# Experts' outputs accumulated in four PSUM banks by float32r one-hot products, picks for two experts at once, one conditional block per expert

## The chip, the cores and the metric

The kernel runs on one core of a Trainium2 chip. The metric is the device time of one execution in microseconds, the median over several runs. An execution under the profiler gives a span (first to last instruction) and its own device time, which is a little above the span.

## The reference

All arithmetic is float32. A first block has two hybrid layers (projections, attention, retention, an mLSTM, output projection). A second block has one layer: a mixer (attention and a gated recurrence), and then a mixture of experts over 256 tokens, which is what the change touches:

```
xn = rms_norm(x, norm2_g)                          # 256 tokens x 1024
logits = xn @ w_router + b_router                  # 32 experts
top_v, top_i = top_k(logits, 4); gates = softmax(top_v)
for each expert e, over the tokens that picked it:
    g = min(xn @ w_gate[e] + b_gate[e], 7)
    u = clip(xn @ w_up[e] + b_up[e], -7, 7)
    y = (g * sigmoid(1.702 g) * (u + 1)) @ w_down[e] + b_down[e]
x = x + sum over a token's 4 experts of gate * y
out = rms_norm(x, final_g)
```

Each of the three weights of an expert is 1024 x 1024 float32, 4 MB, so the 32 experts read 403 MB. 256 tokens with 4 experts each are 32 tokens an expert on average.

## The kernel before

**The first part** (the two layers and the mixer, up to about 480 us) works through weight tiles that are split into two float32r parts, three products each (`mm3`, lines 368 to 370). The change leaves it alone, but for the place at which two buffers are handed back (`give`).

**Weights** come in tiles of 1 MB (128 partitions x 2048 numbers), each by one DMA that SyncE (SP) issues, into a ring of numbered slots (`slot`, tiles named `s`). `give(...)` returns slots and issues the next loads of a list `order` in that order; `release(i)` gives back the slot of load i. In the experts' part 19 slots turn over. An expert uses twelve tiles: four of w_gate, four of w_up, four of w_down.

**One expert** (lines 1303 to 1333) has a capacity of 64 tokens. `pick` makes a one-hot matrix from the tokens' ranks (VectorE), gathers the tokens' rows by float32 matmuls (`xg`), copies them out (ScalarE), transposes them in four 128x128 pieces (`tr`) and scales them into `xT`. `up` multiplies xT by the gate tiles (PSUM bank `g`) and the up tiles (bank `u`). Since only 64 rows of output are wanted, the 128x128 array is used in two halves of 64 columns: matmuls come in pairs that write partitions 0 to 63 and 64 to 127 at the same time. I call this the 64-column form. Each float32 matmul stands in the trace as two instructions (PE) with two weight loads (PEld), so a product of 16 matmuls has 32. The bias is one float32r matmul in the full 128x128 form in the middle of each product. `gated` computes the activation in five steps on VectorE and ScalarE, `down` transposes the result (`tr`), copies it out as `hT` (ScalarE, line 1253) and multiplies by the down tiles (bank `y`). For every two experts `place` builds the transposed and gated one-hot matrices (bank `st`), and `add_pair` multiplies them by the two outputs: four float32 matmuls of 128x512 with two instructions each (bank `cb`), added to x by VectorE (line 1269).

**Experts with over 64 tokens** go through conditional blocks: `more_up` (line 1278) after the first half, `more_down` (line 1284) after the second, nested up to three deep. Every engine loads the expert's token count and branches twice per expert; `foresee` puts a hint for the PE's branch into its stream. In this data two experts take the blocks, expert 1 and expert 29.

**Order.** A scheduler sets the order of the instructions on each engine, so in PE's stream matmuls of one product are interleaved with the picks of the next expert and with the adds. SP's loads for w_gate and w_up stand behind the first conditional block, those for w_down behind the second.

Of the kernel before, what the change touches and what calls it, by code (L numbers as in the profile page):

```python
# [26 lines left out]
def _col_layout():  # L27
    at, off = {}, 0
    for name, n in (
        ("norm0", 8), ("norm1", 8), ("y0", 4), ("y1", 4), ("cw0", 16), ("cw1", 16), ("cb0", 4), ("cb1", 4),  # L30
        ("n1g", 8), ("final", 8), ("cw2", 16), ("cb2", 4), ("ba", 8), ("bi", 8), ("lam", 8), ("og", 8), ("n2g", 8),
    ):
        at[name] = (off, n)
        off += n
    return at, off
# [62 lines left out]
def _prep(i):  # L98
# [29 lines left out]
    z["b_down"] = a["b_down_2"][0][:, :768].reshape(32, 3, 256).transpose(1, 0, 2).reshape(96, 256)  # L128
    z["b_down_end"] = a["b_down_2"][0][:, 768:].reshape(32, 2, 128).transpose(1, 0, 2).reshape(64, 128)
# [21 lines left out]
    put("n2g", a["norm2_g_2"][0])  # L151
    z["cols"] = c
# [43 lines left out]
def _build(tc, T, out):  # L196
# [577 lines left out]
    def mixer(xt):  # L774
# [242 lines left out]
        give(13, 15, 16, 17, 18, 21)  # L1017
# [15 lines left out]
        give(4, 5, 6, 7, 11)  # L1033
# [40 lines left out]
    ew = ctx.enter_context(tc.tile_pool(name="ew", bufs=1))  # L1074
    t22, t23 = slot(22), slot(23)
    xh = slot(12).rearrange("p (a b) -> p a b", a=2)
    bias = ew.tile([128, 1024], F32R, name="bias")
    xg, th = t22[:, 0:512], t22[:, 512:1024]
    more_h = [t22[:, 1024:1536], t22[:, 1536:2048], ew.tile([128, 512], F32, name="more")]
    ys, xTs = ([t23[:, o + 512 * k:o + 512 * k + 512] for k in range(2)] for o in (0, 1024))  # L1080
    nc.scalar.dma_start(rbc[0:96, :], T["b_down"])
    gates, rank = (sm(n, 2, 32, bufs=1) for n in ("gates", "rank"))
    count = small.tile([1, 32], I32, name="count", bufs=1)

    t14 = slot(14)

    def split_bias():

        b = t14[:, 256:1280]
        nc.scalar.dma_start(b, T["bias"])  # L1090
        S.activation(bias, b, AF.Copy)
        for p in (slice(32, 64), slice(96, 128)):
            V.tensor_tensor(bias[p], b[p], bias[p].bitcast(F32), op=OP.subtract)

    def router():
        xT = slot(10).rearrange("p (k t) -> p k t", k=8)
        wr, br = t14[:, 0:256], t14[:, 1536:1568]
        lg, mr = (t14[:, o:o + 72].rearrange("p (a b) -> p a b", a=2) for o in (1568, 1640))
        mask, m8, sel, nv = (t14[:, o:o + n].rearrange("p (a b) -> p a b", a=2)
                             for o, n in ((1712, 64), (1776, 16), (1792, 16), (1808, 4)))  # L1100
        nc.scalar.dma_start(wr, T["w_router"])
        load_row(br, "br")
        r, _ = x_stats(1e-5, xh, False, True)
        tt = [bank(n) for n in ("xg", "tr", "st", "y")]
# [11 lines left out]
        for hf in range(2):  # L1116
            for kt in range(8):
                ins = PE.matmul(t[:, 32 * hf:32 * hf + 32], xT[:, kt, 128 * hf:128 * hf + 128], wr.rearrange("p (k e) -> p k e", k=8)[:, kt, :],
                          start=kt == 0, stop=kt == 7)
            busy(ins, 8 if hf else 4, bank("cb", 2))  # L1120
# [21 lines left out]
        busy(ins, 4, bank("cb", 2))  # L1142
# [4 lines left out]

    def last_bias():

        t = bank("tr")  # L1150
        gx = ew.tile([128, 2, 192], F32, name="hotw")[:, :, 0:96]
        V.tensor_copy(gx.rearrange("p a (q e) -> p a q e", q=3), gates[:, :, None, :].to_broadcast([128, 2, 3, 32]))
        for hf in range(2):
            PE.transpose(t[0:96, 128 * hf:128 * hf + 128], gx[:, hf, :], ident)
        V.tensor_copy(one[0:96, :], t[0:96, 0:256])
        for q, w, o in ((0, rbc, 0), (1, rbc, 256), (2, rbc, 512), (0, b_down, 768), (1, b_down, 896)):
            p, n = slice(32 * q, 32 * q + 32), w.shape[-1]
            t = bank("cb", 2)
            for hf in range(2):
                PE.matmul(t[:, n * hf:n * hf + n], one[p, 128 * hf:128 * hf + 128], w[p, :], start=True, stop=True)  # L1160
            d = x[:, :, o:o + n]
            V.tensor_tensor(d, d, two(t[:, 0:2 * n]), op=OP.add)

    router()
    b_down = before[0:64, :]
    nc.scalar.dma_start(b_down, T["b_down_end"])
    four = lambda v: v.rearrange("p (c s t) -> p c s t", c=4, s=2)
    gain = cols[:, COLS["n2g"][0]:COLS["n2g"][0] + 8].rearrange("p (s c) -> p c s", s=2)

    def ranks(e, j):  # L1170
        if not j:
            return rank[:, :, e]
        r = sm("rj", 2)
        V.tensor_scalar(r, rank[:, :, e], -64.0 * j, None, op0=OP.add)
        return r

    def pick(e, j):

        r = ranks(e, j)
        one_hot = ew.tile([128, 2, 64], F32, name="hot", bufs=2)  # L1180
        for hf in range(2):
            V.tensor_scalar(one_hot[:, hf, :], slots[:, 0:64], r[:, hf:hf + 1], None, op0=OP.is_equal)  # L1182
        t = bank("xg")
        for hf in range(2):
            for c in range(2):
                ins = PE.matmul(t[64 * c:64 * c + 64, :], one_hot[:, hf, :], xh[:, hf, 512 * c:512 * c + 512], start=hf == 0, stop=hf == 1)  # L1186
        S.activation(xg, t, AF.Copy)
        if e + j == 0:
            busy(ins, 2, bank("cb", 2))
        t = bank("tr")  # L1190
        for c in range(4):
            PE.transpose(t[:, 128 * c:128 * c + 128], xg[:, 128 * c:128 * c + 128], ident)
        xT = four(more_h[j - 1] if j else xTs[e % 2])
        V.tensor_tensor(xT, four(t), gain[:, :, :, None].to_broadcast([128, 4, 2, 64]), op=OP.mult)
        return xT

    def place(some, name):

        wt = ew.tile([128, 2, 192], F32, name="hotw")
        rr = [ranks(e, j) for e, j in some]  # L1200
        for hf in range(2):
            for k in range(3 if len(some) == 2 else 1):
                e = some[k % 2][0]
                n = 64 if len(some) == 2 else 128
                V.tensor_scalar(wt[:, hf, 64 * k:64 * k + n], slots[:, 0:n], rr[k % 2][:, hf:hf + 1], gates[:, hf, e:e + 1],
                                op0=OP.is_equal, op1=OP.mult)
        t = bank("st")
        for k in range(len(some)):
            for hf in range(2):
                PE.transpose(t[:, 256 * k + 128 * hf:256 * k + 128 * hf + 128], wt[:, hf, 64 * k:64 * k + 128], ident)  # L1210
        back = ew.tile([128, 256 * len(some)], F32, name=name)
        V.tensor_copy(back, t[:, 0:256 * len(some)])
        return back

    def product(t, a, w, swap=0, mid=None, at=3):
        for i in range(4):
            if i == at and mid:
                mid()
            for k in range(2):
                kt = 2 * i + k  # L1220
                for c in range(2):
                    o = 64 * (c ^ swap)
                    ins = PE.matmul(t[o:o + 64, :], a[:, kt % 4, kt // 4, :], w[i][:, 1024 * k + 512 * c:1024 * k + 512 * c + 512],  # L1223
# [145 lines left out]
```

## Time and profile before

| what | value |
|---|---|
| median of 3 runs | 1562.95 us (1562.74 to 1572.78) |
| profiled execution: time, span | 1557.01 us, 1555.1 us |
| PE busy | 1406.8 us, 90% of the span |
| DVE, ACT busy | 580.6 us (37%), 306.7 us (20%) |
| data moved | 469.31 MB, 302 GB/s over the span |
| granted TensorE clock, mean | 0.979 |

PE is TensorE's matmuls, PEld its weight loads, DVE VectorE, ACT ScalarE, SP the engine that issues the loads. A row of a timeline gives the start, the duration, the engine, the line and the tiles; `x8` says that eight equal instructions were merged in it, and the brackets give the idle time of that engine just before and what ended it. `PEq` or `DVEq` is the engine's own sequencer (a branch, for instance). The distance between the starts of two weight loads tells how long PE really took for one matmul, since ends of matmuls are modelled.

### The profile page before, as it was taken

What the parts mean: (1) busy time and instruction counts of PE and PEld (TensorE: products, weight loads), DVE (VectorE), ACT (ScalarE), POOL (GpSimd) and SP (SyncE); (2) the same over time, 40 slices, a digit from 0 to 9 for tenths busy, and PEclk for the clock granted to TensorE, in tenths of its full rate; (3) what the DMA queues carried; (4) which work ended last, traced back from release to release, by engine and by line L of the source; (5) the groups of instructions that cost most, each with busy time, mean ns of one, the idle gap of its engine ahead of it and who ended that gap; (6) DMA issues with size and microseconds to landing.
All of it is one profiled execution on the core that took longest, in us unless ns stands there. A gap on an engine that the chain in (4) does not pass through costs nothing. (4 is left out here: it accounts for less than half of the span.)

```text
span 1555.1 us, 17575 instructions
## 1 busy us (share of the span) xinstructions
PE 1406.8 (90%) x6638; PEld 707.5 (45%) x6638; DVE 580.6 (37%) x1238; ACT 306.7 (20%) x551; POOL 170.8 (11%) x100
## 2 busy tenths in 40 slices
PE   7899989999879989999899999998999998999896
PEld 6687877888556333333333333333333333333332
DVE  4856467648786212222122212221222222222123
ACT  4335443454552000000000000000000000000001
POOL 3333333344240000000000000000000000000001
PEclk9899999999889999999999999999999999999998
DMA  8423443444258756999999999999999999999561
GB/s 296 160 91 127 137 163 109 142 148 139 81 196 337 297 210 264 419 417 370 412 401 420 407 416 408 377 419 418 417 418 410 419 419 406 413 420 419 235 252 63
DMA packets 67500, 469.31 MB, mean 302 GB/s; under 512 B 8128, under 2 KB 9440, under 8 KB 11744
## 3 DMA queue, kind: packets, MB, share of 16 engines
q1 hardware_dynamic: 65664, 463.38, 74.4%
q8 instruction: 142, 2.33, 0.6%
q10 hardware_dynamic: 1632, 3.10, 0.6%
q14 instruction: 62, 0.51, 0.1%
HBM read 465.40 MB, written 1.05 MB: 300 GB/s over the span
## 5 line engine op out<-in xcount | busy, mean ns | idle before, releaser
L1223 PE MATMUL g<-s,s 128*64 128x512 f32 x1088 | 289.4, 601 | 25.3 <-PEq L1284 23.4
L1223 PE MATMUL y<-s,hT 128*64 128x512 f32 x1088 | 256.5, 602 | 1.8 <-ACT hT L1253 1.8
L1223 PE MATMUL u<-s,s 128*64 128x512 f32 x1088 | 247.5, 596 | 0.0
L1223 PEld LDWEIGHTS g<-s,s 128*64 128x64 f32 x1088 | 83.3, 136 | 179.1 <-issue 175.2
L1223 PEld LDWEIGHTS y<-s,hT 128*64 128x64 f32 x1088 | 91.5, 139 | 148.4 <-issue 124.7
L355 POOL TENSOR_TENSOR s<-s,s 128x1024 fp32r<-128x1024 f32 (+2 forms) x59 | 135.3, 2296 | 215.6 <-ACT s L352 163.5
L1223 PEld LDWEIGHTS u<-s,s 128*64 128x64 f32 x1088 | 74.6, 137 | 142.7 <-issue 139.3
L1328 DVE COPY s<-y 64x512 f32<-64x512 f32 x32 | 22.0, 689 | 297.4 <-ACTq L1284 280.6
L1343 POOL TENSOR_TENSOR s<-x,s 128x512 f32<-128x512 f32 x4 | 4.9, 1266 | 1081.2 <-DVE x L1269 1081.2
L352 ACT ACTIVATE s<-s 128x1024 fp32r<-128x1024 f32 (+2 forms) x100 | 100.0, 1008 | 115.9 <-PE pja L370 54.5
L369 PE MATMUL pjb<-s,s 128*128 128x512 f32 (+2 forms) x288 | 101.1, 351 | 7.6 <-DVE s L355 7.6
L368 PE MATMUL pjb<-s,s 128*128 128x512 f32 (+2 forms) x288 | 102.0, 354 | 1.1 <-ACT s L399 0.7
L368 PE MATMUL pja<-s,s 128*128 128x512 f32 (+2 forms) x272 | 98.8, 364 | 3.1 <-ACT s L352 2.6
L370 PE MATMUL pjb<-s,s 128*128 128x512 f32 (+2 forms) x288 | 100.3, 348 | 1.2 <-DVE s L355 0.8
L369 PE MATMUL pja<-s,s 128*128 128x512 f32 (+2 forms) x272 | 97.4, 358 | 3.6 <-DVE s L355 3.6
L370 PE MATMUL pja<-s,s 128*128 128x512 f32 (+2 forms) x272 | 96.7, 355 | 0.5 <-DVE s L400 0.5
L1245 DVE TENSOR_SCALAR s<-u 128x512 f32<-128x512 f32 x34 | 23.5, 692 | 178.2 <-PE u L1223 178.2
L355 DVE TENSOR_TENSOR s<-s,s 128x1024 fp32r<-128x1024 f32 (+2 forms) x53 | 69.4, 1312 | 52.7 <-ACT s L352 52.5
L1242 DVE TENSOR_SCALAR gm<-g 128x512 f32<-128x512 f32 x32 | 22.1, 692 | 161.4 <-PE g L1223 161.4
L1186 PE MATMUL xg<-s,hot 128*64 128x512 f32 x272 | 78.4, 599 | 2.5 <-DVE hot L1182 2.5
L1243 ACT ACTIVATE s<-gm 128x512 f32<-128x512 f32 x32 | 20.2, 630 | 303.2 <-DVE gm L1242 303.2
L1269 DVE TENSOR_TENSOR x<-x,cb 128x512 f32<-128x512 f32 x72 | 49.1, 687 | 64.9 <-PE cb L1266 64.8
(357 smaller groups left out, 1509.8 us busy)
## 6 DMA issues: line engine op xcount, KB each, us to landing
s<-in_w_up_dram SPq DMA_DIRECT2D x128, 1024.0 KB, 18.0
s<-in_w_gate_dram SPq DMA_DIRECT2D x128, 1024.0 KB, 18.1
s<-in_w_down_dram SPq DMA_DIRECT2D x128, 1024.0 KB, 12.3
s<-in_w_o_dram SPq DMA_DIRECT2D x12, 1024.0 KB, 4.8
s<-in_w_cqk_dram SPq DMA_DIRECT2D x4, 1024.0 KB, 7.9
s<-in_w_bqk_dram SPq DMA_DIRECT2D x4, 1024.0 KB, 4.9
s<-in_w_bvg_dram SPq DMA_DIRECT2D x4, 1024.0 KB, 5.0
s<-in_w_aq_dram SPq DMA_DIRECT2D x4, 1024.0 KB, 4.8
```

The lines of the kernel that those rows point to most:

```text
L352: S.activation(h, w, AF.Copy)
L355: (V if el == "V" else G).tensor_tensor(lo, w, h.bitcast(F32), op=OP.subtract)
L368: PE.matmul(d, ah, bh, start=start, stop=False, skip_group_check=True)
L369: PE.matmul(d, ah, bl, start=False, stop=False, skip_group_check=True)
L370: PE.matmul(d, al, bh, start=False, stop=stop, skip_group_check=True)
L1186: ins = PE.matmul(t[64 * c:64 * c + 64, :], one_hot[:, hf, :], xh[:, hf, 512 * c:512 * c + 512], start=hf == 0, stop=hf == 1)
L1223: ins = PE.matmul(t[o:o + 64, :], a[:, kt % 4, kt // 4, :], w[i][:, 1024 * k + 512 * c:1024 * k + 512 * c + 512], start=kt == 0, stop=kt == 7)
L1242: V.tensor_scalar(gm, tt[0], 7.0, None, op0=OP.min)
L1243: S.activation(th, gm, AF.Tanh, scale=0.851)
L1245: V.tensor_scalar(th, tt[1], 7.0, -7.0, op0=OP.min, op1=OP.max)
L1269: V.tensor_tensor(d, d, t[c], op=OP.add)
L1328: cp(ys[c][p, :], t[p, :])
```

## The change

- Four PSUM banks (`a00` to `a11`, one for each half of the tokens and of the columns) hold the sum of all experts' outputs to the end. `last_bias` (now in expert 0 rather than in expert 6) starts them with gate-weighted b_down; `scatter` adds an expert by eight float32r matmuls with 64 rows (K = 64); x is added once, after the last expert. `add_pair` and its additions to x are gone.
- An output y leaves PSUM scaled by the token's gate, as two float32r parts (`down`, ScalarE and VectorE). `places` makes the one-hot matrix for it directly in transposed form, by one float32r matmul that spreads the row of ranks and two tiny ones that fetch the gate (`m2`), instead of transposes (`place`).
- `pick` multiplies the tokens as the stationary side by a one-hot matrix of two experts, so xT comes out transposed; the copy `xg` and the four transposes go. Half of a pair's picks (eight matmuls of 128x128, 16 instructions, bank `m1`) is done in each expert.
- One conditional block, `more` (line 1298), which stands between the transposes of the activation and the down product, takes the place of the two. The down product ends without a branch; its slots are released behind no conditional.
- The eviction of the transposed activation is split between ScalarE and VectorE (`turned`).
- Slots 10 and 14 are handed back in the mixer, before the experts' part rather than in it.

```diff
-    def add(lhs, rhs):
-        for hf in range(2):
-            t = [bank("cb", 2) for _ in range(2)]
-            for c in range(2):
-                PE.matmul(t[c], lhs(c, hf), rhs(c), start=True, stop=True)
-            for c in range(2):
-                d = x[:, hf, 512 * c:512 * c + 512]
-                V.tensor_tensor(d, d, t[c], op=OP.add)
...
+    def one_hots(b):
+
+        for hf in range(2):
+            V.tensor_tensor(hot[:, hf], rank[:, hf, 2 * b:2 * b + 2, None].to_broadcast([128, 2, 64]),
+                            slots[:, None, 0:64].to_broadcast([128, 2, 64]), op=OP.is_equal)
...
+    def places(e, j):
+
+        t = bank("m2")
+        PE.matmul(t[:, 0:256], idr[:, e:e + 1].to_broadcast([32, 128]), rT, start=True, stop=True)
+        for hf in range(2):
+            PE.matmul(t[:, 256:258], hotm[:, hf, :], gp[:, hf, e, :], start=hf == 0, stop=hf == 1)
...
+        V.tensor_scalar(back, t[:, 0:256], -64.0 * j, col("slotp", 0), op0=OP.add, op1=OP.is_equal)
+        return g, back
+
+    def pick(b, q):
+
+        t = bank("m1").rearrange("p (k n) -> p k n", k=4)
+        for i in range(4):
+            kt = 4 * q + i
             for hf in range(2):
...
+                PE.matmul(t[:, i, :], xh[:, hf, 128 * kt:128 * kt + 128], hot[:, hf].rearrange("p e s -> p (e s)"), start=hf == 0, stop=hf == 1)
+        V.tensor_tensor(xTs[b % 2][:, 4 * q:4 * q + 4, :], t, gain[:, 4 * q:4 * q + 4, None].to_broadcast([128, 4, 128]), op=OP.mult)
...
+    def turned(h, d):
+
+        t = bank("g").rearrange("p (c s t) -> p c s t", c=4, s=2)
...
+        S.activation(d[:, 0:2], t[:, 0:2], AF.Copy, scale=0.5)
+        V.tensor_scalar(d[:, 2:4], t[:, 2:4], 0.5, None, op0=OP.mult)
+        return lambda kt: d[:, kt % 4, kt // 4, :]
+
+    def down(a, w, g):
+
+        t = bank("u")
+        product(t, a, w[8:12])
+        yp = yw(F32R)
+        S.activation(yp[0], t, AF.Copy, scale=g)
+        V.scalar_tensor_tensor(yp[1], t, g, yp[0].bitcast(F32), op0=OP.mult, op1=OP.subtract)
+        return yp
+
+    def scatter(back, yp, stop=False):
+
+        for hf in range(2):
+            for k in range(2):
+                for c in range(2):
+                    p = slice(64 * c, 64 * c + 64)
+                    PE.matmul(total[hf][c], back[p, 128 * hf:128 * hf + 128], yp[k][p, :], start=False, stop=stop and k == 1,
+                              skip_group_check=True)
...
-    def more_up(e, w, n, j):
-
-        with tc.If(n > CAP * j, label=f"up{e}_{j}"):
-            gated(up(e, pick(e, j), w), xg, more_h[j - 1])
+    def more(e, own, w, n, j):
+
+        with tc.If(n > CAP * j, label=f"more{e}_{j}"):
+            xT, hm = yw(F32)
+            xT = pick_more(e, j, xT)
+            t = up(own, lambda kt: xT[:, kt, :], w)
+            g, back = places(e, j)
+            gated(t, hm)
+            scatter(back, down(turned(hm, hTm), w, g))
             if j < 3:
...
+        t = up(own, lambda kt: xT[:, kt, :], w, f"more{e}_1")
+        gated(t, hid)
+        one_hot(e, 0)
+        if not e:
             last_bias()
+        if b < 15:
+            pick(b + 1, i)
+        g, back, before_it = *places(e, 0), back
+        if e:
+            scatter(before_it, yp)
+        a = turned(hid, hT)
         n = nc.values_load(count[0:1, e:e + 1], min_val=0, max_val=256)
-        more_up(e, w, n, 1)
+        more(e, own, w, n, 1)
         for k in range(8):
             release(i0 + k)
...
+        yp = down(a, w, g)
         for k in range(8, 12):
             release(i0 + k)
-    add_pair()
...
+    scatter(back, yp, True)
```

PE before, in the second half of an expert with an add (expert 16; `xg` the pick, `cb` the add, `tr` the transposes of the pick):

```order
L1223 MATMUL u<-s_11329,s_3959 64x512 x4
L1223 MATMUL u<-s_11331,s_3959 64x512 x4
L1223 MATMUL u<-s_11333,s_3959 64x512 x4
L1234 MATMUL u<-bias,own 128x512
L1223 MATMUL u<-s_11606,s_3959 64x512 x4
L1186 MATMUL xg<-s_3960,hot 64x512 x4
L1266 MATMUL cb<-s_3959,back 128x512
L1192 MATMUL tr<-cst,s_3958 128x128 x4
L1266 MATMUL cb<-s_3959,back 128x512 x3
L1320 TENSOR_LOAD count
L1278 COMPARE_AND_BRANCH
```

The four u blocks stand nearly together and the pick and the add follow them, ahead of the branch.

PE after the change, the same place; this order stands in experts 4 to 26 (`m_11246` is bank m2, `a_4103` to `a_4106` are a00 to a11):

```order
L1241 MATMUL u<-s_10717,s_3966 64x512 x4
L1249 MATMUL u<-bias,own 128x512
L1202 MATMUL m_11246<-rT,idr 128x256
L1204 MATMUL m_11246<-gp,hotm 128x2 x2
L1288 MATMUL a_4103<-yw,back 128x512
L1288 MATMUL a_4104<-yw,back 128x512
L1288 MATMUL a_4103<-yw,back 128x512
L1288 MATMUL a_4104<-yw,back 128x512
L1288 MATMUL a_4105<-yw,back 128x512
L1241 MATMUL u<-s_11146,s_3966 64x512 x4
L1288 MATMUL a_4106<-yw,back 128x512
L1288 MATMUL a_4105<-yw,back 128x512
```

Ahead of these rows stand a u block, two matmuls of the pick (`m1`), a second u block and six matmuls of the pick; behind them one more scatter matmul, the four transposes of the activation (into bank g), and the load of the count and the branch at line 1298. So the u product is cut into four blocks with picks and scatters between them, five of the eight scatter matmuls stand ahead of its last block, and the transposes of the activation have moved ahead of the branch.

PE after the change in experts 1, 2 and 27 to 29:

```order
L1241 MATMUL u<-s_16824,s_3966 64x512 x4
L1241 MATMUL u<-s_16826,s_3966 64x512 x4
L1241 MATMUL u<-s_16828,s_3966 64x512 x4
L1249 MATMUL u<-bias,own 128x512
L1241 MATMUL u<-s_17255,s_3966 64x512 x4
L1219 MATMUL m_17347<-hot,s_3968 128x128 x8
L1202 MATMUL m_17357<-rT,idr 128x256
L1204 MATMUL m_17357<-gp,hotm 128x2 x2
```

Here the whole u product comes first, and the pick, the places and all eight scatters stand between it and the transposes. Experts 30 and 31 are the same without the pick.

## Rows read from the trace of the kernel before

**Rows 1.** Page, part 1: busy time, share of the span, instructions.
```profile
PE 1406.8 (90%) x6638; PEld 707.5 (45%) x6638; DVE 580.6 (37%) x1238; ACT 306.7 (20%) x551; POOL 170.8 (11%) x100
```

**Rows 2.** Windows: stretch, PE, PEld, DVE, ACT, POOL busy, clock, DMA share, GB/s.
```profile
520.00:560.00 40.00, 36.89 (x167) 12.74 (x164) 8.88 (x20) 3.04 (x5) 0.00 (x0) 1.00 0.68 281
640.00:680.00 40.00, 37.98 (x160) 13.30 (x161) 7.45 (x13) 3.59 (x6) 0.00 (x0) 1.00 1.01 417
...
1000.00:1040.00 40.00, 38.54 (x171) 13.53 (x170) 8.15 (x14) 3.64 (x6) 0.00 (x0) 1.00 1.01 420
...
1480.00:1520.00 40.00, 37.82 (x153) 13.00 (x152) 11.04 (x21) 2.42 (x4) 0.00 (x0) 1.00 0.62 240
```

**Rows 3.** Timeline, ACT: the hT eviction of experts 0, 2, 28 and 31.
```profile
516.49 0.60 ACT L1253 ACTIVATE hT<-tr 128x512 f32<-128x512 f32 x1 [2.80 <-PE tr L1251]
...
610.35 0.60 ACT L1253 ACTIVATE hT<-tr 128x512 f32<-128x512 f32 x1 [4.29 <-PE tr L1251]
...
1410.13 0.60 ACT L1253 ACTIVATE hT<-tr 128x512 f32<-128x512 f32 x1 [5.43 <-PE tr L1251]
...
1531.10 0.60 ACT L1253 ACTIVATE hT<-tr 128x512 f32<-128x512 f32 x1 [9.42 <-PE tr L1251]
```

**Rows 4.** Page, part 6: the loads of one expert weight (the others alike).
```profile
s<-in_w_up_dram SPq DMA_DIRECT2D x128, 1024.0 KB, 18.0
```

**Rows 5.** Timeline, PEld: end of an u product with its bias.
```profile
1005.46 0.14 PEld L1223 LDWEIGHTS u<-s,s 128*64 128x64 f32 x2 [0.29 <-issue]
1005.89 0.14 PEld L1223 LDWEIGHTS u<-s,s 128*64 128x64 f32 x2 [0.28 <-issue]
1006.85 0.19 PEld L1234 LDWEIGHTS u<-bias,own 128*128 128x128 f32 x1 [0.81 <-issue]
1007.27 0.20 PEld L1223 LDWEIGHTS u<-s,s 128*64 128x64 f32 x4 [0.24 <-issue]
...
1008.61 0.14 PEld L1186 LDWEIGHTS xg<-s,hot 128*64 128x64 f32 x2 [0.29 <-issue]
```

**Rows 6.** Timeline, PEld: float32 matmuls of 128x128, 16 instructions, and the next row.
```profile
488.22 1.87 PEld L1057 LDWEIGHTS cb<-one 128*128 128x128 f32 x16
490.01 0.30 PEld L1137 LDWEIGHTS u<-s,cst 128*128 128x128 f32 x2
```

**Rows 7.** Timeline, PEld: two float32r matmuls of 128x512 in the first part.
```profile
340.86 0.19 PEld L369 LDWEIGHTS pjb<-s,s 128*128 128x128 f32 x1
341.09 0.19 PEld L370 LDWEIGHTS pjb<-s,s 128*128 128x128 f32 x1
```

**Rows 8.** Timeline, PE: float32 matmuls with 64 rows in the conditional add.
```profile
586.18 1.25 PE L1266 MATMUL cb<-s,backm 64*128 64x512 f32 x4
```

**Rows 9.** Timeline, PEld: last loads of an u product, then transposes of the activation.
```profile
668.21 0.14 PEld L1223 LDWEIGHTS u<-s,s 128*64 128x64 f32 x2 [0.29 <-issue]
671.08 0.42 PEld L1251 LDWEIGHTS tr<-cst,gm 128*128 128x128 f32 x4 [2.72 <-issue]
```

**Rows 10.** Timeline, PEld: four transposes, the branch at line 1278, the next load.
```profile
1072.04 0.42 PEld L1192 LDWEIGHTS tr<-cst,s 128*128 128x128 f32 x4 [0.41 <-ACT s L1187]
1073.60 0.42 PEld L1251 LDWEIGHTS tr<-cst,gm 128*128 128x128 f32 x4 [1.14 <-PEq L1278]
```

**Rows 11.** Lines 1284 and 1278: PE's branches, ns min/median/max; who waited for line 1284.
```profile
L1284 PEldq COMPARE_BRANCH  x36: 87/1706/6497, 523.3 to 1534.4; - x36
...
  PE g L1223: 23.4, 29
...
L1278 PEldq COMPARE_BRANCH  x36: 74/422/3322, 514.3 to 1526.3; - x36
```

**Rows 12.** Timeline, PEld: loads around the branch at line 1284.
```profile
1053.48 0.17 PEld L1223 LDWEIGHTS g<-s,s 128*64 128x64 f32 x2 [0.26 <-issue]
1056.17 0.23 PEld L1223 LDWEIGHTS g<-s,s 128*64 128x64 f32 x4 [2.53 <-issue]
```

**Rows 13.** Timeline, PE: the last add of the kernel.
```profile
1540.39 3.86 PE L1266 MATMUL cb<-s,back 128*128 128x512 f32 x8 [1.56 <-DVEq L1284]
```

More of the change, by code (lines that the diff above doesn't have):

```diff
@@ L1080, in _build, with yw @@
[L1080 to L1085, printed above, removed]
+    def yw(dt):
+        t = ew.tile([128, 1024], dt, name="yw")
+        return t[:, 0:512], t[:, 512:1024]
+    raw = ew.tile([128, 1024], F32, name="yw")
     def split_bias():
-        b = t14[:, 256:1280]
-        nc.scalar.dma_start(b, T["bias"])
-        S.activation(bias, b, AF.Copy)
+        S.activation(bias, raw, AF.Copy)
@@ L1167, in _build @@
[L1167 to L1183, printed above, removed]
+            PE.transpose(t[0:32, 128 * hf:128 * hf + 128], gates[:, hf, :], ident)
@@ L1184, in pick @@
+        V.tensor_copy(gT, t[0:32, 0:256])
         for hf in range(2):
             for c in range(2):
[L1186 to L1193, printed above, removed]
@@ L1194, in pick @@
-        V.tensor_tensor(xT, four(t), gain[:, :, :, None].to_broadcast([128, 4, 2, 64]), op=OP.mult)
-        return xT
[L1197 to L1213, printed above, removed]
@@ L1216, in product @@
+    def product(t, a, w, mid=None):
         for i in range(4):
-            if i == at and mid:
+            if i == 3 and mid:
                 mid()
@@ L1233, in up @@
             tt.append(t)
[L1234 to L1235 removed]
+            product(t, xT, w[4 * m:4 * m + 4], lambda: PE.matmul(t, own, bias[:, 512 * m:512 * m + 512], start=False, stop=False,
+                                                                 skip_group_check=True))
             if label and not m:
@@ L1248, in down @@
-    def down(h, w, swap=0, label=None):
-        t = bank("tr")
+        V.scalar_tensor_tensor(h, th, 1.0, h, op0=OP.add, op1=OP.mult)
+    def turned(h, d):
+        t = bank("g").rearrange("p (c s t) -> p c s t", c=4, s=2)
+        d = d.rearrange("p (c s t) -> p c s t", c=4, s=2)
         for c in range(4):
-            PE.transpose(t[:, 128 * c:128 * c + 128], h[:, 128 * c:128 * c + 128], ident)
-        hT = ew.tile([128, 4, 2, 64], F32, name="hT")
-        S.activation(hT, four(t), AF.Copy, scale=0.5)
-        t = bank("y")
-        mid = None
-        if label:
-            mid = lambda: foresee(label, last[0])
-        ins = product(t, hT, w[8:12], swap, mid, 1)
-        last[0] = ins
-        return t
@@ L1274, in foresee @@
             tc.mark_branch_hint_location(label, hint="LikelyTaken", engines=[mybir.EngineType.PE])
-    def more_up(e, w, n, j):
-        with tc.If(n > CAP * j, label=f"up{e}_{j}"):
-            gated(up(e, pick(e, j), w), xg, more_h[j - 1])
-            if j < 3:
-                more_up(e, w, n, j + 1)
-    def more_down(e, w, n, j):
-        with tc.If(n > CAP * j, label=f"down{e}_{j}"):
-            y = more_h[j - 1]
-            t = down(y, w)
-            busy(last[0], 4, bank("cb", 2))
-            S.activation(y, t, AF.Copy)
-            back = place([(e, j)], "backm")
-            half = lambda c: slice(64 * c, 64 * c + 64)
-            add(lambda c, hf: back[half(c), 128 * hf:128 * hf + 128], lambda c: y[half(c), :])
-            if j < 3:
-                more_down(e, w, n, j + 1)
-    cur = pick(0, 0)
+    def more(e, own, w, n, j):
[6 more added lines that the diff above has]
+            scatter(back, down(turned(hm, hTm), w, g))
+            if j < 3:
+                more(e, own, w, n, j + 1)
+    one_hots(0)
+    rank_rows()
+    for q in range(2):
+        pick(0, q)
     split_bias()
-    give(10, 14)
     back = None
-    def add_pair():
-        add(lambda c, hf: back[:, 256 * c + 128 * hf:256 * c + 128 * hf + 128], lambda c: ys[c])
+    fr = t22[:, 0:1024]
     for e in range(32):
```

147 lines of the change are left out of this document (81 added, 66 removed).

## The prediction

> **What bounds the kernel now.** I read the page first: PE is busy for 90% of the span [rows 1]. An average over stages can't say which limit holds where, so I took the windows next, by the stage that the change touches. From 520 to 640 us the DMA queues are busy for about two thirds of the time; from 640 to 1440 they are full, at 417 to 420 GB/s; from there on they are at 60% [rows 2]. PE is at about 38 of 40 us in all of these. So two limits lie close together. I then measured each alone.
>
> The loads: twelve tiles of 1 MB an expert [rows 4] are 12.58 MB, and at 418 GB/s that is 30.1 us.
>
> The instructions: from expert 2 to expert 28 the hT evictions are 1410.13 - 610.35 = 799.8 us apart [rows 3], that is 30.76 us for each of 26 experts. Among PE's waits in that stretch the loads do not appear. So **PE's own chain sets the pace, and the loads stand only 2% below it.** That decides what the change can be worth: between experts 2 and 28 a faster PE soon meets the loads. Ahead of expert 2 and behind expert 28 it does not.
>
> **How PE's time is counted.** I go by the distance between weight loads. In the 64-column form a pair of instructions takes 0.43 us (1005.46 to 1005.89) [rows 5]. An expert's three products are 96 instructions, 48 pairs, 20.6 us, before and after. Where another form follows, its first load comes 0.96 us after the last pair instead of 0.43, so the array runs empty first; the return is quicker than usual, since two pairs are loaded together. From the last pair through the bias and four more pairs it is 1008.61 - 1005.89 = 2.72 us against 2.15 for five pairs [rows 5]. The bias itself holds PE for 0.42 of that, so a round trip costs what stands in it plus 0.15 us.
>
> **One expert after the change** (experts 4 to 26), from one down product to the next:
> - 48 pairs: 20.6 us. Bias of g: 0.57.
> - Pick: 16 instructions of 128x128 float32. Sixteen such take 1.79 us [rows 6], with the drains at the ends of two blocks and two returns 2.6.
> - Bias of u, places, five scatters: the bias 0.42; places 0.5 to 0.6 (three short matmuls at the spacing of rows 6, and drains). The scatters' form, 64 rows in float32r, is nowhere in the trace. From above: 0.23 us each one behind the other, the spacing of full float32r matmuls [rows 7]. From below: half, two side by side, as in the 64-row float32 matmuls, where four instructions end in 1.25 us [rows 8] though one behind the other they would stream for four times 0.43. I take side by side, as rows 8 have the same shape: 0.75 with its drain; the other end adds 0.9 over all eight. With the return 1.9.
> - The end: the activation needs 2.87 us from the last u load to the transposes [rows 9]. Three scatters lie in that gap and cost nothing; if they ran longer, they would have 1 us of room. From transposes through the branch to the next load it is 1.56 us [rows 10]: I take 1.8, as both halves of hT must be out too. Less the last pair, which is counted, and the quick return: 3.75.
>
> Sum 29.4 us, against 30.76. What has gone is the `xg` pick with its transposes, the float32 adds, the transposes of `place`, and the second branch: there PE waits 23.4 us in all [rows 11] and its load stream stands still for up to 2.5 us at a time [rows 12]. In experts 1, 2 and 27 to 29 pick, places and scatters fill the wait for the activation, and the same accounting gives 27.5 us; without a pick (30, 31) 25.4.
>
> VectorE and ScalarE get about as much as they lose and have their work done ahead of u's end; I cost it at nothing, the cover being u's four blocks. If `back` or the scaled y were late, the scatters would hold up the last u block. The loads of w_gate and w_up still follow the one conditional on SP; those of w_down no longer wait for a second and come earlier.
>
> **The sum**, against the profiled span of 1555.1 us:
> - Up to expert 0's hT: two picks one behind the other through one bank instead of one, 1.7 us; the four float32 matmuls of the biases move here from expert 6, 3.4 us with their transposes' wait. +5.
> - Expert 0's hT to expert 2's: 93.9 us before [rows 3]. After it is 27.5 twice and expert 1's block. Its up half is 15 us, the wait for the activation 2.5, its down half 6.5, its pick (32 instructions) 3.5; evictions, scatters, and two passes through branches make the rest of 36 (33 to 40). 91: -3.
> - Expert 2 to 28: PE alone would take 26 x 29.4 = 764 us. The loads would take 26 x 30.1 = 783, less what the buffers hold at the start: of 19 slots up to 11 are full when eight have just been freed, 28 us of lead, so 755 to 783. Two limits so close wait for each other now and then; I take 29.8 us, 775. Against 799.8: -25.
> - Expert 28 to 31: 121.0 us before [rows 3]; 27.5 + 36 + 25.4 + 25.4 = 114. -7.
> - The end: eight float32 instructions of the last add, 3.86 us behind a branch [rows 13], become eight scatters of about 1 us and a second eviction. -1.
>
> Together -31: a span of 1524 us. The profiled execution's time is 1.9 us over its span, and the median of the runs 5.9 us over that: **1532 us**.
>
> **Rivals.**
> 1. *Every change of form costs the whole drain.* Place: the cut u product in each expert. The change adds eight changes of form (four around the two pick blocks, four from places through the scatters to u and back). At the full 0.53 us of rows 5 and without the quick return these are 4.2 us, of which my sum holds 1.2: 32.4 us an expert. At that pace PE alone sets it: experts 2 to 28 take 842 us, 67 over my 775, six others 3 us more each, and the median is about 1617 us. Half of it gives 1569; slower by over 1% begins at 1.8 us an expert more than my 29.4. For it: the drain is there in every such row. Against: the quick return in rows 5, and rows 8. Chance 0.11. The Trainium skill, "TensorEngine Tiling (Array Packing)", Key Properties, says that a change of tiling mode drains TensorE, which speaks against this change; the trace agrees on the drain (0.96 against 0.43 us) and takes part of it back at the return.
> 2. *The one branch that is left becomes dear, or the loads have no lead.* At line 1284 PE's branch takes 1.7 us in the median and up to 6.5; at line 1278 0.42 [rows 11]. Line 1284's hint stands early in the down product, line 1278's some ten microseconds ahead. The new one's hint stands like line 1278's, but nothing hides what its branch takes, as it comes behind the transposes. One more microsecond an expert gives 30.4 us, 790 from 2 to 28 and 6 elsewhere, about 1553 us; without any lead of the loads 783 from 2 to 28, 1540. The Trainium skill, "Runtime: NRT & Kernel Launch", Instruction fetch mechanics, says that a taken branch beyond the fetched window waits for a DMA; line 1284's long branches, at full DMA queues, agree with it. Chance 0.27, for 1540 to 1560.
> 3. *The loads are faster than I think, or the lead is whole:* 755 us, and the block 33: about 1515. Chance 0.05.
>
> The granted clock is 1.00 in these windows [rows 2], the upper level; PE's idle stretches get no longer with the change, so I cost it at nothing.
>
> **The numbers.** The forecast (1520 to 1545) has 0.57, rival 2 0.27, rival 1 0.11, rival 3 0.05. The range goes from 1518 to 1556 us: below, the lead nearly whole and a cheap block; above, rival 2 nearly whole. A measurement tells about 1%, here 15.6 us, from no change. Faster than 1547 is all of the forecast, rival 3, and 0.09 of rival 2: 0.71. Within 1%: the rest of rival 2: 0.18. Slower: rival 1: 0.11.
>
> **What would show it.** In the profile after: hT evictions 29 to 30 us apart between experts 4 and 26, and DMA share near 1.00 from about 620 us to the last loads; in experts 27 to 31 under 28 us; two loads of scatters within 0.15 us of each other; next y load 1.6 to 1.9 us after the transposes; the first hT some 5 us later. Wrong if the scatters are 0.23 us apart throughout, if the gap from transposes to y is over 3 us, or if PE waits for loads while the DMA share is under 0.95.

## The result, and the profile after

The changed kernel takes 1575.28 us (median of 20 runs, 1564.48 to 1590.86), the kernel before 1565.03 us in the runs beside it. The ratio is 1.0064, 95% interval 1.0036 to 1.0092: 0.6% slower, where I forecast 1532 us. A second set of runs gave 1585.89 us and a ratio of 1.0133 (1.0085 to 1.0182).

The page of one execution after, part 1 (busy time, share, instructions), answers to [rows 1], and the view of cores adds the mean granted clock:

```profile
PE 1434.0 (90%) x6930; PEld 771.3 (49%) x6930; DVE 544.1 (34%) x1216; ACT 282.7 (18%) x517; POOL 171.3 (11%) x100
...
core 0: 1585.4 us, clock 0.933
```

Before, the clock of the profiled execution was 0.979. PE's share is the same 90%, so that number alone would say that nothing happened. The windows, answering to [rows 2] (stretch, PE, PEld, DVE, ACT and POOL busy, granted clock, DMA share, GB/s), say more:

```profile
520.00:560.00 40.00, 37.26 (x146) 14.93 (x144) 6.43 (x13) 2.33 (x4) 0.00 (x0) 0.83 0.50 204
640.00:680.00 40.00, 34.76 (x156) 13.10 (x154) 6.22 (x15) 2.24 (x4) 0.00 (x0) 0.96 1.01 420
1000.00:1040.00 40.00, 37.72 (x176) 15.42 (x172) 8.48 (x21) 2.33 (x4) 0.00 (x0) 0.96 0.98 396
1400.00:1440.00 40.00, 38.37 (x186) 15.29 (x184) 8.36 (x18) 3.02 (x5) 0.00 (x0) 1.00 1.01 420
1480.00:1520.00 40.00, 35.66 (x175) 14.35 (x176) 6.53 (x14) 2.39 (x4) 0.00 (x0) 1.00 0.36 136
```

In [rows 2] the clock is 1.00 everywhere. After, it is not, until about 1400 us. The hT evictions of experts 0, 2, 28 and 31 (timeline of ACT, as [rows 3]; the eviction is at line 1269 now):

```profile
539.03 0.38 ACT L1269 ACTIVATE s<-g 128x256 f32<-128x256 f32 x1 [16.09 <-PE g L1268]
...
635.72 0.38 ACT L1269 ACTIVATE s<-g 128x256 f32<-128x256 f32 x1 [10.39 <-PE g L1268]
...
1449.41 0.38 ACT L1269 ACTIVATE s<-g 128x256 f32<-128x256 f32 x1 [10.40 <-PE g L1268]
...
1561.11 0.38 ACT L1269 ACTIVATE s<-g 128x256 f32<-128x256 f32 x1 [8.40 <-PE g L1268]
```

The stages, as measured against [rows 3] and against the forecast:

| stage | before | forecast | after |
|---|---|---|---|
| to expert 0's hT | 516.5 | 521.5 | 539.0 |
| hT of expert 0 to 2 | 93.9 | 91 | 96.7 |
| hT of expert 2 to 28 | 799.8 | 775 | 813.7 |
| hT of expert 28 to 31 | 121.0 | 114 | 111.7 |
| behind it | 24.0 | 23 | 24.3 |
| span | 1555.1 | 1524 | 1585.4 |

Most of the miss is in one row, experts 2 to 28: 38.7 us. Its evictions are 31.0 to 31.5 us apart in most experts and 32.7 in some, where I had 29.4 for PE alone. From expert 27 on, where the u product is no longer cut, they are 27.9 and 27.6 us apart, as forecast.

One expert of the slow kind in the timeline of PEld (start, duration, line, operation, idle time before and what ended it), from the end of u over the last three scatters and the transposes into y:

```profile
914.67 0.14 PEld L1241 LDWEIGHTS u<-s,s 128*64 128x64 f32 x2 [0.28 <-issue]
915.62 0.29 PEld L1288 LDWEIGHTS a<-yw,back 64*128 64x128 f32 x3 [0.81 <-issue]
917.27 0.42 PEld L1268 LDWEIGHTS g<-cst,s 128*128 128x128 f32 x4 [1.36 <-issue]
919.23 0.33 PEld L1241 LDWEIGHTS u<-s,s 128*64 128x64 f32 x4 [1.53 <-ACTq L1298]
920.14 0.27 PEld L1241 LDWEIGHTS u<-s,s 128*64 128x64 f32 x2 [0.59 <-issue]
920.99 0.27 PEld L1241 LDWEIGHTS u<-s,s 128*64 128x64 f32 x2 [0.59 <-issue]
921.85 0.27 PEld L1241 LDWEIGHTS u<-s,s 128*64 128x64 f32 x2 [0.59 <-issue]
922.43 0.16 PEld L1241 LDWEIGHTS u<-s,s 128*64 128x64 f32 x2 [0.32 <-issue]
922.86 0.16 PEld L1241 LDWEIGHTS u<-s,s 128*64 128x64 f32 x2 [0.27 <-issue]
```

The first pairs of y (tile u again) come 0.85 us apart, twice the usual 0.43, and from 922.4 on 0.43. The windows around it show the reason in the column before the DMA share:

```profile
912.00:915.60 3.60, 3.60 (x17) 1.45 (x16) 0.62 (x3) 0.00 (x0) 0.00 (x0) 1.00 1.01 421
915.60:918.70 3.10, 1.38 (x9) 0.71 (x7) 1.70 (x3) 0.38 (x1) 0.00 (x0) 1.00 0.86 357
918.70:922.10 3.40, 2.84 (x8) 1.11 (x10) 0.73 (x4) 0.00 (x0) 0.00 (x0) 0.51 0.82 284
922.10:930.00 7.90, 7.90 (x38) 2.82 (x37) 0.75 (x1) 0.69 (x1) 0.00 (x0) 1.00 1.00 418
```

PE was busy for 1.38 of 3.10 us, waiting for the activation and then, behind the transposes, for their eviction and the branch; the clock then stood at half, the lower of its two levels (1.2 GHz), for 3.4 us, just as y began. Between the hT of experts 2 and 28 there are 22 such stretches, each 3.4 or 6.8 us long, 92 us together. Before there were two in that stage, 6.8 us.

### The profile page after: what moved, and what is told of

Same layout as the page of the kernel before. It is cut to its first block, busy times and chain, and to the rows that moved or that the text cites. A ratio compares the mean times of both kernels' runs of the same rounds, so it can differ in the third digit from the quotient of the medians.

```text
span 1585.4 us, 17668 instructions
## 1 busy us (share of the span) xinstructions
PE 1434.0 (90%) x6930; PEld 771.3 (49%) x6930; DVE 544.1 (34%) x1216; ACT 282.7 (18%) x517; POOL 171.3 (11%) x100
## 5 line engine op out<-in xcount | busy, mean ns | idle before, releaser
L1241 PE MATMUL u<-s,s 128*64 128x512 f32 x2112 | 530.6, 645 | 50.2 <-DVEq L1298 40.6
L1241 PEld LDWEIGHTS u<-s,s 128*64 128x64 f32 x2112 | 164.4, 147 | 335.2 <-issue 294.2
L1241 PE MATMUL g<-s,s 128*64 128x512 f32 x1024 | 233.4, 595 | 0.0
L1279 DVE SCALAR_TENSOR_TENSOR yw<-u,gj,yw 128x512 fp32r<-128x512 f32 x32 | 24.0, 751 | 287.0 <-ACT yw L1278 287.0
L1257 DVE TENSOR_SCALAR s<-g 128x512 f32<-128x512 f32 x32 | 22.1, 692 | 190.6 <-PE g L1241 190.6
L1219 PEld LDWEIGHTS m<-hot,s 128*128 128x128 f32 x512 | 63.0, 195 | 44.6 <-issue 44.4
L1278 ACT ACTIVATE yw<-u,gj 128x512 fp32r<-128x512 f32 x32 | 22.0, 687 | 314.5 <-PE u L1241 314.5
L1219 PE MATMUL m<-hot,s 128*128 128x128 f32 x512 | 73.6, 291 | 0.2 <-DVE s L1220 0.2
L369 PEld LDWEIGHTS pjb<-s,s 128*128 128x128 f32 x288 | 57.6, 200 | 15.4 <-DVE s L355 8.6
L1258 ACT ACTIVATE s<-s 128x512 f32<-128x512 f32 x32 | 20.2, 630 | 246.4 <-DVE s L1257 246.4
```

What stands on the lines that cost most here:

```text
L369: PE.matmul(d, ah, bl, start=False, stop=False, skip_group_check=True)
L1219: PE.matmul(t[:, i, :], xh[:, hf, 128 * kt:128 * kt + 128], hot[:, hf].rearrange("p e s -> p (e s)"), start=hf == 0, stop=hf == 1)
L1241: last[0] = PE.matmul(t[o:o + 64, :], a(kt), w[i][:, 1024 * k + 512 * c:1024 * k + 512 * c + 512], start=kt == 0, stop=kt == 7)
L1257: V.tensor_scalar(h, tt[0], 7.0, None, op0=OP.min)
L1258: S.activation(th, h, AF.Tanh, scale=0.851)
L1278: S.activation(yp[0], t, AF.Copy, scale=g)
```

## The experiments

The theory after this reading: **the granted clock falls once per expert where the u product is cut**, since pick and five of the scatters don't fill PE's wait for the activation, and this costs the 39 us. Rival A: the changes of form cost more than I took (my first rival). Rival B: the loads get only about 400 GB/s beside this kernel. Later rival C came up, that the clock doesn't matter to the time. All runs' views below are one window in the middle of the experts, 700 to 1390 us, with the columns as above; the kernel after stands first, a second trace of it reads the same in clock and GB/s:

```profile
700.00:1390.00 690.00, 637.00 (x2835) 252.96 (x2834) 132.41 (x306) 37.40 (x66) 0.00 (x0) 0.94 0.98 401
```

**1. Fill the wait: eight matmuls of ones behind the scatters.**

```diff
         if e:
-            scatter(before_it, yp)
+            busy(scatter(before_it, yp), 8, bank("m2"))
```

(`busy` is the kernel's own helper; `scatter` returns its last instruction here.)

> Eight matmuls of ones (128x128 float32, results unused) are put behind the last scatter of each expert, where TensorE now waits 1.54 us for the activation. Theory (the granted clock: the thin stretch from places to y lets it fall to the lower level for 3.4 to 6.8 us once per expert between experts 3 and 26): the stretches at 0.50 between 660 and 1400 us go from 23 to under 6, hT evictions of experts 4 to 26 come 30.1 to 30.7 us apart instead of 31.45, and the median is about 1552 us (1545 to 1560). Rival A (the changes of form cost more than I took): eight more instructions in the same form fill idle time and change nothing, 1575 us, hT 31.4 us apart, or a little more. Rival B (loads: the queues give only 400 GB/s beside this kernel): 1575 us, DMA share stays at 0.97 whatever the clock.

Measured: 1575.47 us, ratio to before 1.0087 (1.0052 to 1.0121). The window:

```profile
700.00:1390.00 690.00, 648.40 (x3210) 288.79 (x3206) 134.81 (x309) 37.42 (x66) 0.00 (x0) 0.99 0.99 405
```

The clock came back (3 falls from expert 2 to 28 instead of 22), and the evictions are 30.4 to 30.8 us apart, as the theory had it, yet the time is the same: the miss that made rival C worth a test. Two things in the trace account for it. The fillers are too many: from the last scatter to the transposes it is now 2.33 us instead of 1.54, 0.8 us an expert (from the transposes to y it is 2.0 or 2.3 us in turn, in the kernel after too). And three branches have become long, 4.1 to 5.7 us from the last transpose to y instead of about 2; the three falls stand right behind them (PEld's timeline at one of them; the view of line 1299, the conditional block's line in this kernel, ns min/median/max):

```profile
707.12 0.47 PEld L1268 LDWEIGHTS g<-cst,s 128*128 128x128 f32 x4
713.13 0.33 PEld L1241 LDWEIGHTS u<-s,s 128*64 128x64 f32 x4 [5.53 <-issue]
```
```profile
L1299 PEldq COMPARE_BRANCH  x36: 74/360/5934, 519.5 to 1544.6; - x36
```

The stage from expert 2 to 28 still takes 806.6 us, so this run doesn't decide.

**2. The same with four matmuls, which fit into the wait.** The edit is as above with 4 for 8.

> As the kernel with eight matmuls of ones behind the scatters, but four: by the traces four are 8 weight loads 0.11 us apart, 0.9 us, in a gap of 1.54 us of which 0.55 goes before the first, so they should cost nothing. Theory (the granted clock): experts 4 to 26 without a 0.50 stretch take TensorE's own 29.5 us or the loads' 30.1, against 30.4 to 30.7 with eight and 31.0 to 32.7 with none; if four keep the clock up, median 1538 to 1548 us; if they do so in half of the experts, 30.7 on the mean and 1550 to 1562. Rival A (changes of form): 31.4 us apart and 1575 us. Rival C (the clock costs nothing, since with eight fillers it was up and the time the same): 1575 us.

Measured: 1553.86 us, ratio 0.9938 (0.9906 to 0.9971). The timeline of PEld at the same place of an expert, and the window:

```profile
1015.66 0.14 PEld L1241 LDWEIGHTS u<-s,s 128*64 128x64 f32 x2 [0.29 <-issue]
1016.61 0.29 PEld L1288 LDWEIGHTS a<-yw,back 64*128 64x128 f32 x3 [0.81 <-issue]
1017.27 0.97 PEld L1057 LDWEIGHTS m<-one 128*128 128x128 f32 x8 [0.37 <-issue]
1018.27 0.42 PEld L1268 LDWEIGHTS g<-cst,s 128*128 128x128 f32 x4
1020.55 0.23 PEld L1241 LDWEIGHTS u<-s,s 128*64 128x64 f32 x4 [1.86 <-issue]
1021.03 0.17 PEld L1241 LDWEIGHTS u<-s,s 128*64 128x64 f32 x2 [0.26 <-issue]
```
```profile
700.00:1390.00 690.00, 652.49 (x3165) 281.58 (x3163) 140.81 (x324) 39.20 (x70) 0.00 (x0) 1.00 1.01 419
```

Its hT evictions of experts 2 and 28 (timeline of ACT):

```profile
629.50 0.38 ACT L1269 ACTIVATE s<-g 128x256 f32<-128x256 f32 x1 [11.32 <-PE g L1268]
...
1407.05 0.38 ACT L1269 ACTIVATE s<-g 128x256 f32<-128x256 f32 x1 [11.34 <-PE g L1268]
```

This decides. The order of the instructions is that of the kernel after, cuts and changes of form and all, with 31 times four useless matmuls on top, and it is 21 us faster. From last scatter to transposes it is still 1.54 us. No fall is left between experts 2 and 28; the evictions stand 29.5 to 29.9 us apart in 21 of the 26 experts (28.9 in one) and the stage takes 777.5 us. Rival A would have kept 31.4 us, rival B 400 GB/s, rival C the time. Of the four that take longer (30.5 to 31.6 us) three stop for 1.4 to 1.8 us within y, which no wait in the trace explains; the fourth has another order. The median stays above the 1538 to 1548 that I expected; in the profiled execution 10 us of that lie ahead of the experts (their first hT at 532.9, not 522.7).

**3. Pick, places and scatters behind the whole u product in every expert**, as the changed kernel has it in experts 1, 2 and 27 to 29 (the four calls are indented under one line):

```diff
+        with tc.issue_after(last[0].ins):
             ...
             if b < 15:
                 pick(b + 1, i)
             g, back, before_it = *places(e, 0), back
             if e:
                 scatter(before_it, yp)
```

> Pick, places and scatters of every expert are held behind the last matmul of the u product, as the order already is in experts 1, 2 and 27 to 29; nothing else changes. Theory (the clock): no 0.50 stretches between 660 and 1400 us, as there are none now between 1397 and 1574; hT 30.1 to 30.7 us apart (the loads' pace) and the median 1545 to 1556 us. Rival A (changes of form): faster too, since two cuts of u go, by 4 drains of about 0.5 us, 2 us an expert, down to the loads' pace; but then the clock in 660 to 1400 us may stay at 0.94 as now. Rival B (loads): unchanged, 31.4 us an expert, 1575 us, because TensorE waits for u's weights where it did the pick before.

Measured: 1539.94 us, ratio 0.9843 (0.9801 to 0.9884). The window, and PE's waits between the hT of experts 2 and 28 (us in total, times, longest):

```profile
700.00:1390.00 690.00, 622.73 (x2976) 252.86 (x2977) 139.54 (x326) 39.15 (x69) 0.00 (x0) 1.00 1.01 420
```
```profile
PE u L1241 <- DVEq L1298: 38.9, 26, 1.7
PE u L1241 <- DMA s<-in_w_up_dram: 29.4, 59, 1.5
```

No fall, 773.2 us for the stage, the loads at 420 GB/s, and PE now waits for them (29.4 us): rival B is out. Rival A can't be told from the theory by this time alone.

**4. Which cut matters.** Two halves of experiment 3: only pick behind u, with the scatters still cutting it; and only places and scatters behind u, with pick still cutting it. The edits put the same line over one or the other.

> Only pick is held behind the u product; places and scatters still cut u twice. Theory: pick's dense 2 us lie in the wait for the activation, so no 0.50 stretches between 700 and 1400 us, hT at the loads' pace of 30.1 to 30.4 us, median 1537 to 1548 us. Rival A (changes of form dear): two cuts remain, four changes more than with the whole u product first; if each costs 0.5 us fully, 27.6 + 2 = 29.6 us, hidden by the loads, the same time; if they cost more, above 1550.

> Places and scatters are held behind the u product; pick still cuts u twice, and nothing dense is left for the wait for the activation. Theory: the thin stretch (last u load to y) is about 5 us, nearer to the kernel before (2.9 + 0.6 + 0.8 us) than to the changed one (7 us); so some stretches at 0.50 appear, 3 to 15 between 700 and 1400 us, hT 30.2 to 30.9 us, median 1542 to 1562 us. Rival A (changes of form dear): pick's four changes stay, 1555 to 1575 us with the clock at 1.00.

Measured: 1542.57 us (0.9829, 0.9765 to 0.9893) and 1539.59 us (0.9822, 0.9761 to 0.9882), four runs each. The windows, one of each kernel:

```profile
700.00:1390.00 690.00, 636.34 (x3005) 253.43 (x3003) 140.41 (x324) 39.83 (x70) 0.00 (x0) 1.00 1.01 420
```
```profile
700.00:1390.00 690.00, 633.07 (x2990) 251.68 (x2986) 138.91 (x325) 39.74 (x70) 0.00 (x0) 1.00 1.01 420
```

Either half is enough. In the second I had expected some falls and there were none, with 4.65 to 5.00 us from u's last load to y's first: eight scatters and three matmuls of places are enough to fill it. Two cuts with all their changes of form cost nothing that can be seen here, since the loads cover them. What ends rival A is experiment 2, which has all the cuts and still takes 29.5 to 29.9 us an expert.

**5. The other way: make PE idle longer in the kernel of experiment 3.** Three passes of VectorE over h, which leave its values as they are:

```diff
         gated(t, hid)
+        for _ in range(3):
+            V.scalar_tensor_tensor(hid, hid, 1.0, hid, op0=OP.mult, op1=OP.max)
```

> Whole u product first in every expert, as in the kernel that took 1540 us, plus three passes of VectorE over h (0.69 us each in the trace, values unchanged), which make TensorE idle 2.1 us longer ahead of the transposes. TensorE's chain would be about 27.6 + 2.1 = 29.7 us, still under the loads' 30.1. Theory (the clock): the stretch from scatters to y gets as thin as in the changed kernel, 10 to 22 stretches at 0.50 appear in experts 4 to 26, and each puts its 1.4 us on top: 30.6 to 31.4 us, median 1555 to 1575 us. Rival A and rival B (no part of the clock in it): hidden by the loads, 30.1 us and 1540 to 1545 us.

Measured: 1550.02 us, ratio 0.9929 (0.9891 to 0.9967).

```profile
700.00:1390.00 690.00, 634.62 (x3002) 260.96 (x2998) 181.40 (x393) 39.81 (x70) 0.00 (x0) 0.98 1.01 420
```

Idling alone, with no cut, brings the falls: 10 from expert 2 to 28 instead of none, though PE idles only about 0.5 us longer there (1.8 to 2.2 us from u's last load to y's first, not 1.3 to 1.6), since pick and scatters cover the rest of the three passes. But that stage still takes 774.6 us: PE was ahead of the loads, and they hide what the falls cost. I had put the cost on top of the loads' pace, and that was wrong. Against experiment 3 its trace is longer ahead of the experts (first hT at 532.9, not 522.7) and behind the loads (28 to 31: 126.3 us, not 120.6), where nothing covers PE; there the passes cost as well as the falls.

**6. The sum in float32**, four products per expert instead of eight, once in the order of the kernel after and once in that of experiment 3:

```diff
-        yp = yw(F32R)
+        yp = yw(F32)
         S.activation(yp[0], t, AF.Copy, scale=g)
-        V.scalar_tensor_tensor(yp[1], t, g, yp[0].bitcast(F32), op0=OP.mult, op1=OP.subtract)
...
-        back = ew.tile([128, 256], F32R, name="back" + k, bufs=1 if j else 2)
+        back = ew.tile([128, 256], F32, name="back" + k, bufs=1 if j else 2)
...
-            for k in range(2):
-                for c in range(2):
+            for c in range(2):
```

> The sum of the experts' outputs with four float32 one-hot products per expert instead of eight in float32r, y scaled once by ScalarE without the second part; the order stays cut as in the changed kernel. Theory (the clock): each product streams about four times as long, so less of the wait for the activation is empty; the 0.50 stretches get rarer (23 down to 5 to 15), hT 30.5 to 31.2 us apart, 1555 to 1570 us. Rival A (changes of form): as many changes and about 0.8 us more of products: 31.5 to 32.2 us apart, 1575 to 1590 us. Rival B (loads): unchanged, 1575 us.

> Whole u product first in every expert, and the sum in four float32 products per expert instead of eight in float32r. Theory: the loads bound experts 4 to 26 at 30.1 us whichever form the sum has, so 1536 to 1544 us, as with float32r; the float32r form is worth nothing there. If the form of the sum matters by itself, as the 13 us between the two cut kernels (1575 and 1562) might say, up to 13 us less than 1540.

Measured: 1562.24 us (1.0008, 0.9977 to 1.0039) in the cut order, 13 us less than the kernel after; 1549.04 us (0.9901, 0.9863 to 0.9938) with the whole u product first. The windows:

```profile
700.00:1390.00 690.00, 643.79 (x2906) 254.03 (x2908) 121.70 (x299) 37.84 (x67) 0.00 (x0) 0.97 1.00 412
```
```profile
700.00:1390.00 690.00, 637.85 (x2997) 259.80 (x2992) 121.23 (x300) 39.79 (x70) 0.00 (x0) 1.00 1.01 420
```

In the cut order the falls are halved, 11 of 22, and the evictions alternate: 30.0 us in experts without a fall, 31.4 with one. That is the clearest price of a single fall, 1.4 us. The kernel after has it too: of these three evictions the first two are 29.9 us apart, with no fall between them, the next two 31.0, with one of 3.4 us; where a fall is 6.8 us long it is 32.7.

```profile
700.53 0.38 ACT L1269 ACTIVATE s<-g 128x256 f32<-128x256 f32 x1 [12.31 <-PE g L1268]
730.39 0.38 ACT L1269 ACTIVATE s<-g 128x256 f32<-128x256 f32 x1 [12.31 <-PE g L1268]
761.42 0.38 ACT L1269 ACTIVATE s<-g 128x256 f32<-128x256 f32 x1 [12.32 <-PE g L1268]
```

The float32r form gains nothing by itself here: it made PE's work shorter where PE had to wait anyway. In the second kernel the stage takes 772.7 us, as expected; that its median is 9 us over experiment 3 lies ahead of the experts in the trace (first hT at 536.8).

**7. A version that beats both**: experiment 3 with six matmuls of ones at the head of the conditional block, where PE waited 1.6 us and the clock then fell (`busy(None, 6, bank("m2"))` as the block's first line).

> Whole u product first in every expert, and six matmuls of ones at the head of the conditional block of experts 1 and 29, where TensorE waits about 1.6 us and the clock then falls for 6.8 and 10.2 us in the trace of the kernel with the whole u product first. Theory: both stretches go or get shorter; six are 1.3 us in a wait of 1.6, so they cost nothing; 3 to 7 us less than 1540: 1533 to 1538. If the wait there is not filled but lengthened, 1540 to 1543.

Measured: 1533.94 us, ratio to before 0.9834 (0.9798 to 0.9871). Its stages are 523.8, 92.1, 773.6, 118.6 and 24.0 us, the span 1532.2. In the trace the two stretches in the block have gone, and expert 0 to 2 takes 92.1 us instead of 95.4. In the time this can't be told from experiment 3, whose ratio to before is 0.9843: the kernel before was 5 us faster in these runs, too.

**8. The kernel after once more**, for a second trace.

> The changed kernel a second time, for a second trace. Theory: stretches at 0.50 once per expert in experts 3 to 26 again, hT 31.0 to 31.6 us apart, experts 27 and 28 below 29 us with none; 1565 to 1590 us, depending on how long the clock is at the lower level in the part ahead of the experts (85 us in the first trace, 51 us in the trace of the kernel before). If the fall was an accident of one run, few stretches and 1535 to 1545.

Measured: 1585.89 us. Again 22 falls and 92 us at half, again 813.7 us from expert 2 to 28. The falls belong to the program and not to one execution.

## Why the prediction was wrong

**The step that failed** is the one sentence on the clock: "PE's idle stretches get no longer with the change, so I cost it at nothing." No single idle stretch gets longer, but there are two now where there was one. Expert 12 before and expert 11 after, from u's last load to y's first (the window as above, then rows of PE's timeline; tile u after the change is y):

```profile
918.33:922.59 4.26, 2.39 (x12) 0.74 (x9) 1.94 (x5) 0.60 (x1) 0.00 (x0) 1.00 0.98 379
921.21 0.63 PE L1251 MATMUL tr<-cst,gm 128*128 128x128 f32 x4 [1.87 <-DVEq L1278]
921.77 1.20 PE L1186 MATMUL xg<-s,hot 128*64 128x512 f32 x2
```
```profile
914.67:919.23 4.56, 2.31 (x13) 0.86 (x10) 1.94 (x4) 0.38 (x1) 0.00 (x0) 0.95 0.87 341
917.31 0.63 PE L1268 MATMUL g<-cst,s 128*128 128x128 f32 x4 [0.95 <-DVE s L1261]
919.26 2.79 PE L1241 MATMUL u<-s,s 128*64 128x512 f32 x5 [1.32 <-DVEq L1298]
```

Before, PE idles 1.87 us ahead of the transposes, and two matmuls of the pick fill the wait behind them; after, it idles 0.95 us ahead of them and 1.32 behind. And this expert before is not the usual one: from expert 15 on picks and adds fill the wait, and PE idles 0.9 to 1.3 us in it, against 1.7 to 1.9 in experts 3 to 13 and 2.2 to 2.9 in experts 3 to 26 after. The clock falls 22 times after and twice before, both times in experts 3 to 13, and with the wait filled (experiment 2), or with pick or all the scatters left in it (experiments 3 and 4), it doesn't fall at all. The change put the pick and five of the scatters where they cut u, and left three scatters in the wait; I had counted that as a matter of drains alone. The price is 813.7 - 777.5 = 36.2 us for 22 falls, five of them 6.8 us long (experiment 2 against the kernel after), 1.6 us each, near the 1.4 of experiment 6. Of the 43 us between forecast and median this is nearly all; the rest are small terms of both signs.

Point by point:
- *PE's sum of 29.4 us per expert*: right. With the clock up the same order runs at 29.5 to 29.9 us (experiment 2). Of its terms, the way from the transposes to y came out at 2.0 to 2.3 us, where I took 1.8, and the wait for the activation at 2.6, where I took 2.87. The scatters stand side by side as I took from rows 8: three loads in 0.29 us.
- *Expert 2 to 28 in 775 us, loads and PE both near the limit*: right for the clock that I assumed. Six kernels without or nearly without falls took 772.5 to 777.5 us there.
- *27.5 us in experts 27 to 29*: right, 27.6 to 27.9. *28 to 31 in 114 us*: 111.7.
- *First hT 5 us later*: 6.2 in the executions whose first part has the clock of before (522.7 in experiments 1, 3 and 6). The 539.0 of the table holds some 16 us more, in the part ahead of the experts, which the change leaves as it was; that part varies by itself (below).
- *Expert 0 to 2 in 91 us*: 96.7; the clock falls there too, 10.2 us. With the block's wait filled it is 92.1 (experiment 7).
- *Rival 1, drains*: wrong; at 32.4 us an expert it is 2.5 us and more over experiment 2.
- *Rival 2, the one branch becomes dear*: not in this kernel. PE's compare takes 348 ns in the median and 457 at most, where [rows 11] had up to 6497:

```profile
L1298 PEldq COMPARE_BRANCH  x36: 74/348/457, 535.6 to 1560.8; - x36
```

  In experiment 1, with eight more matmuls an expert, three long branches come back. None of my rivals held the clock; the one that ended slower had the wrong mechanism. Nor did my signs of being wrong look at it: neither the distance of the scatters nor the gap from transposes to y came out as the sign that I had named.

The Trainium skill, "TensorE: Matmul & The Clock Gate", A second HAM failure mode: psum-queue depth-cycling, says of another kernel, which cycles through PSUM banks, that PE's short idles between groups of matmuls came often enough to make its clock swing between the two levels, and that the loss is in throughput between the bursts. This trace agrees that short idles go with a swinging clock: PE is busy for 637 of 690 us, and the clock is at 0.94; its idles are waits for the activation, the transposes' eviction and the branch.

How much PE idles from u's last load to y's first goes with the number of falls in these kernels: none in the 14 experts before with 0.9 to 1.3 us, nor in experiments 2, 3 and 4 with 1.3 to 1.7 (experts 4 to 28); 2 falls in the 11 experts before with 1.7 to 1.9; 10 in 27 experts of experiment 5 and 11 in 23 of experiment 6's cut order, both with 1.8 to 2.2; 22 in the 24 after with 2.2 to 2.9. What stays open is which expert is hit. In experiment 6 those with 1.85 us are hit and those with 2.2 are not, turn about, and expert 14 before idles 3.1 us in one stretch without a fall.

## What to carry to other kernels

When a change takes work out of one of TensorE's waits, or parts one wait into two, cost the clock of what comes behind, and read the granted clock in windows as short as the wait, since PE's busy share was 90% before and after. Where the order is free, leave dense work for the wait (here pick and scatters behind the whole u product, 35 us); where it isn't, a few useless matmuls that fit into the wait gave 21 us. And a slower PE cost time here only where the loads weren't the limit: ten falls cost nothing visible between experts 2 and 28 in experiment 5.

## What the runs showed of the hardware

Useless matmuls can pay: four of them, 0.9 us an expert and all of it in a wait, took away falls of 1.6 us each.

PE's branches were long in one kernel and short in the next: between experiments 1 and 2, which differ only by four matmuls an expert, the longest passage from the last transpose to y went from 5.7 us to 2.1 (expert 0 apart). The long ones come about 250 us apart (707, 958 and 1206 us), as the stops within y in experiment 2 come 269 us apart (815, 1084 and 1353 us). What sets either off wasn't tried.

The part ahead of the experts (up to 520 us) has the clock at half for 51 us in some traces and for 72 to 85 in others, in one or two stretches of 20.5 us that the others lack. The first 500 us of the kernel after and of experiment 3:

```profile
0.00:500.00 500.00, 446.42 (x2426) 368.88 (x2426) 322.02 (x666) 218.81 (x401) 166.42 (x96) 0.91 0.42 151
```
```profile
0.00:500.00 500.00, 444.67 (x2548) 369.81 (x2550) 332.47 (x717) 220.48 (x405) 166.65 (x96) 0.96 0.46 164
```

Expert 0's hT is up to 16 us later where they stand. The runs of the kernel after spread by 26 us in the first set, with the mean clock from 0.930 to 0.951, the slower mostly the lower. How much of that spread the long stretches make, and what sets them off, is open: each run but the profiled one has only a time and a mean clock.
